# One layer of a hybrid decoder on one core: the first transfers held to three at a time

## The chip, the core and the metric

The kernel runs on one core of one Trainium2 chip. The metric is device microseconds of one execution. Before the change three runs gave 461.85, 461.92 and 461.99 us, median 461.92. The engines named below are TensorE (PE; its weight loads are PEld), VectorE (DVE), ScalarE (ACT), GpSimd (POOL) and SyncE (SP), whose queue issues nearly all transfers.

## The reference, cut to what matters

```
proj = x @ w_in                                  # 256 x 2048 by 2048 x 6656, split in nine parts
q_mo, k_mo = rope(q_mo), rope(k_mo)              # rotary from `positions`
y_mo = causal_softmax_attention(q_mo, k_mo, v_mo) * silu(g_mo)      # 8 heads x 128
y_gm = gelu(u) * (tril(W_s) @ layer_norm(gelu(v)) + b_s) * silu(g_gm)   # 4 groups x 128
mem_k, mem_v = split(mem @ w_mem_kv)             # 256 memory tokens, 2048 x 1024
y_me = softmax_attention(q_me, mem_k, mem_v) * silu(g_me)           # 4 heads x 128
out = layer_norm(ALPHA * x + concat(y_mo, y_gm, y_me) @ w_out)
```

All data are float32. With 256 positions there is one block of keys, so the block-sparse attention is plain causal attention.

## The kernel before

Every large product is computed with operands split into a high part `hi` (rounded by ACT, `split`, lines 106 to 108) and a rest `lo = raw - hi` (DVE, line 108); the products hi·hi, lo·hi and hi·lo are added up in PSUM.

The weights come as one stream of pieces in the order in which TensorE uses them (`STREAM`, line 41). The first item, "H", is `mem @ w_mem_kv` for the values: 16 pieces, one for each 128 rows of the contraction. A piece of H (array `head`) holds 256 columns of the transposed memory and 512 columns of weights, 128 x 768 floats, 384 KB. `load_piece` (lines 135 to 157) takes a buffer of the tag `wraw` (six of them, shared by `hraw` and `wraw`), has SP issue the transfer, and splits both halves: ACT makes `memX` hi (line 150; DVE for the first piece, line 148) and `whi`, DVE makes `memX` lo (line 151) and `wlo`. `whi` and `wlo` have four buffers each.

`next_pieces` (line 191) calls `load_piece` for the piece that is due and three more (`LEAD`). `proj_n` (line 220) runs six matmuls of 512 columns for each piece of H, in the order hi·hi, hi·lo of the memory, lo of the weights, for two token tiles (lines 242 to 246). Then `proj_t` (line 202) computes four blocks of `mem_k` from the same memory; in those calls a hook (line 441) loads the eight pieces of `xT` (`load_act`, line 172, 256 KB each, split into `xX`) and, once, calls `rotary()` (line 273), which loads `pos` and `inv_freq` and computes the tables `sinT` and `cosT` with some twenty DVE instructions and two ACT sines. `xX` and the tables are used only after those four blocks. The rest is the input projections, the attention, the gate units and the output projection with its layer norm.

Before the first piece TensorE runs seven matmuls on zeros (`N_WARM`, line 121).

What sets the order on each engine is not the text alone. The kernel is written for a framework that traces it and then orders all instructions itself: it runs through them with its own estimates of time and lets each engine take the ready instruction that stands first in the text; where the next one in the text is not ready by its estimate, a later one may go first. It also places all semaphore waits and gives tiles their buffers. Each engine then runs its own list strictly in that order.

Of the kernel before, what the change touches and what calls it, by code (L numbers as in the profile page):

```python
# [9 lines left out]
F32 = mybir.dt.float32  # L10
# [7 lines left out]
P = 128  # L18
S = 256
D = 2048  # L20
KT = D // P
# [33 lines left out]
PIECE = 1024  # L55
LEAD = 3
N_WARM = 7


def pieces_of(item):  # L60

    if item[0] == "H":
        return KT, 1, item[3]
    width = P if item[0] == "T" else item[3]
    kts = PIECE // width
    return KT // kts, kts, width
# [14 lines left out]
def hymba_layer(ctx: ExitStack, tc: tile.TileContext, xT, head, x, pos, inv_freq, w, wsT, b_s,  # L81
                gln_g, gln_b, ln_g, ln_b, out):
    nc = tc.nc

    def pool(name, bufs, space=None):
        kw = {"space": space} if space is not None else {}
        return ctx.enter_context(tc.tile_pool(name=name, bufs=bufs, **kw))
# [3 lines left out]
    wp = pool("wp", 1)  # L91
# [8 lines left out]
    def f32(ap):  # L100
        return ap.bitcast(F32)
# [4 lines left out]
    def split(hi, lo, src):  # L106
        nc.scalar.activation(hi, src, AF.Copy)  # L107
        nc.vector.tensor_tensor(out=lo, in0=src, in1=f32(hi), op=ALU.subtract)  # L108
# [10 lines left out]
    idle = ps_side.tile([P, NW], F32, tag="side", name="idle")  # L119
    for _ in range(N_WARM):  # L120
        nc.tensor.matmul(idle, zero[:, :P], zero, start=True, stop=True)
# [3 lines left out]
    for i, item in enumerate(STREAM):  # L125
        n, kts, width = pieces_of(item)
# [3 lines left out]
    for n, (i, j, _, _) in enumerate(pieces):  # L130
        if j == 0:
            first_piece[i] = n
    ready = {}

    def load_piece(n):
        if n >= len(pieces) or n in ready:
            return
        i, j, kts, width = pieces[n]
        if i == len(STREAM) - 1 and j > LEAD:
            hi, lo = (held_home(j - LEAD - 1, b).rearrange("p (k n) -> p k n", k=kts) for b in range(2))  # L140
        else:
            hi = wp.tile([P, kts, width], F32R, tag="whi", name="whi", bufs=LEAD + 1)
            lo = wp.tile([P, kts, width], F32R, tag="wlo", name="wlo", bufs=LEAD + 1)
        if STREAM[i][0] == "H":
            both = wp.tile([P, PIECE], F32, tag="wraw", name="hraw", bufs=6)[:, :S + width]
            nc.sync.dma_start(both, head[j])
            if j == 0:
                nc.vector.tensor_copy(memX[:, j, 0, :], both[:, :S])
            else:
                nc.scalar.activation(memX[:, j, 0, :], both[:, :S], AF.Copy)  # L150
            nc.vector.tensor_tensor(out=memX[:, j, 1, :], in0=both[:, :S], in1=f32(memX[:, j, 0, :]), op=ALU.subtract)
            split(hi[:, 0, :], lo[:, 0, :], both[:, S:])
        else:
            raw = wp.tile([P, kts, width], F32, tag="wraw", name="wraw", bufs=6)
            nc.sync.dma_start(raw, w[n - KT].rearrange("p (k n) -> p k n", k=kts))
            split(hi, lo, raw)
        ready[n] = (hi, lo)
# [3 lines left out]
    def held_home(m, b):  # L161

        if m < 2:
            return outX[0][:, 2 * m + b, :]
        tag, pool_ = (("mv", act), ("pT", work))[m - 2]
        return pool_.tile([P, 2, NW], F32R, tag=tag, name="held", bufs=2).rearrange("p a n -> p (a n)")
# [24 lines left out]
    def next_pieces(hook=None):  # L191
        i = item[0]
        item[0] += 1
        n, kts, width = pieces_of(STREAM[i])
        for j in range(n):
            for m in range(LEAD + 1):
                load_piece(first_piece[i] + j + m)
            if hook is not None:
                hook(j)
            yield j, kts, ready.pop(first_piece[i] + j)  # L200
# [430 lines left out]
```

## Time and profile before

| | us |
|---|---|
| median of three runs | 461.92 |
| the profiled execution | 462.48 |
| its span, first to last instruction | 460.8 |
| PE busy in the span | 447.7 |
| DVE, ACT busy | 343.1, 231.4 |

TensorE is busy for 97% of the span; its own work and the short start and end around it make up the time. The profiled execution takes 1.7 us more than its span, and 0.56 us more than the median of the runs. Times in the trace are microseconds from the start of the span. The column of the granted clock reads 1.00 in the first microseconds, where the trace has no record of it.

### The profile page before, as it was taken

How to read it: one execution, taken by the hardware profiler on the slowest of the kernel's cores; microseconds unless marked ns; L12 is line 12 of the kernel's file. 1: busy time of each engine (PE TensorE's matmuls, PEld its weight loads, DVE VectorE, ACT ScalarE, POOL GpSimd, SP SyncE). 2: the span in 40 equal slices, each digit the busy share in tenths (PEclk: the TensorE clock that was granted, in tenths of full speed). 3: DMA queues.
4: the chain of work that ended last, by engine and by line, in shares of the span. 5: the costliest groups of instructions: out<-in, count | busy, mean ns of one | idle time of the engine just before them, and what ended most of it. 6: DMA issues, size and time to landing. Idle time of an engine off the chain costs nothing.

```text
span 460.8 us, 6498 instructions
## 1 busy us (share of the span) xinstructions
PE 447.7 (97%) x2367; PEld 381.9 (83%) x2367; DVE 343.1 (74%) x592; ACT 231.4 (50%) x369; POOL 6.6 (1%) x17
## 2 busy tenths in 40 slices
PE   8999999999999999999999999999999999999990
PEld 4888888888888888888888888888888888888880
DVE  5989865777577988885678888867987746466666
ACT  5876854575444555554455455445655543336200
POOL 1000000000000000000000000000100000000000
PEclk9999999999999999999999999999999999999996
DMA  8988786544455445544555455966464557676122
GB/s 286 351 338 301 269 273 229 164 166 148 158 197 181 163 170 184 182 160 169 195 185 177 168 184 174 313 213 214 158 213 177 184 191 236 205 231 209 70 91 91
DMA packets 28543, 91.77 MB, mean 199 GB/s; under 512 B 3296, under 2 KB 3424, under 8 KB 28512
## 3 DMA queue, kind: packets, MB, share of 16 engines
q1 hardware_dynamic: 27936, 90.32, 56.7%
q10 hardware_dynamic: 576, 1.05, 0.6%
q8 instruction: 18, 0.29, 0.2%
q14 instruction: 13, 0.11, 0.1%
HBM read 89.26 MB, written 2.10 MB: 198 GB/s over the span
## 4 chain that ended last, share of the span: by engine, by line
PE 96%; DMA 1%; DVE 1%; ACT 0%; issue 0%; SPq 0%; DVEq 0%
PE acc L210 36%; PE acc L211 18%; PE acc L112 11%; PE acc L114 11%; PE acc L113 11%; PE acc L245 4%; DMA hraw<-head 1%; PE ptp L405 1%; PE sc L112 1%; DVE hX L557 0%; DVE hX L553 0%; PE pv L114 0%; PE sc L113 0%; PE pv L113 0%; PE sc L114 0%; PE pv L112 0%
## 5 line engine op out<-in xcount | busy, mean ns | idle before, releaser
L108 DVE TENSOR_TENSOR wlo<-wraw,whi 128x1024 fp32r<-128x1024 f32 x140 | 171.3, 1224 | 79.8 <-ACT whi L107 78.6
L210 PE MATMUL acc<-xX,whi 128*128 128x512 f32 x640 | 227.3, 398 | 0.0
L107 ACT ACTIVATE whi<-wraw 128x1024 fp32r<-128x1024 f32 x140 | 148.3, 1059 | 150.4 <-PE acc L210 60.3
L211 PE MATMUL acc<-xX,wlo 128*128 128x256 f32 x640 | 179.4, 280 | 0.0
L210 PEld LDWEIGHTS acc<-xX,whi 128*128 128x128 f32 x640 | 120.1, 188 | 27.8
L211 PEld LDWEIGHTS acc<-xX,wlo 128*128 128x128 f32 x640 | 120.9, 189 | 0.1
L112 PE MATMUL acc<-whi,yX 128*128 128x512 f32 x112 | 43.6, 389 | 0.0
L114 PE MATMUL acc<-wlo,yX 128*128 128x512 f32 x112 | 43.6, 389 | 0.0
L113 PE MATMUL acc<-whi,yX 128*128 128x512 f32 x112 | 43.6, 389 | 0.0
L112 PE MATMUL acc<-whi,xX 128*128 128x512 f32 x96 | 38.1, 396 | 0.0
L114 PE MATMUL acc<-wlo,xX 128*128 128x512 f32 x96 | 37.5, 391 | 0.0
L113 PE MATMUL acc<-whi,xX 128*128 128x512 f32 x96 | 37.5, 390 | 0.0
L114 PEld LDWEIGHTS acc<-wlo,yX 128*128 128x128 f32 x112 | 21.0, 188 | 4.4
L113 PEld LDWEIGHTS acc<-whi,yX 128*128 128x128 f32 x112 | 21.0, 188 | 4.4
L112 PEld LDWEIGHTS acc<-whi,yX 128*128 128x128 f32 x112 | 21.0, 188 | 4.3
L210 PE MATMUL acc<-memX,whi 128*128 128x512 f32 x64 | 22.6, 399 | 0.0
L114 PEld LDWEIGHTS acc<-wlo,xX 128*128 128x128 f32 x96 | 18.0, 188 | 3.9
L112 PEld LDWEIGHTS acc<-whi,xX 128*128 128x128 f32 x96 | 18.1, 188 | 3.4
L113 PEld LDWEIGHTS acc<-whi,xX 128*128 128x128 f32 x96 | 18.1, 188 | 3.4
L245 PE MATMUL acc<-whi,memX 128*128 128x512 f32 x64 | 17.8, 400 | 0.9 <-ACT whi L107 0.9
L217 DVE TENSOR_TENSOR projT<-acc,part 128x256 f32<-128x256 f32 x44 | 18.1, 414 | 0.0
L211 PE MATMUL acc<-memX,wlo 128*128 128x256 f32 x64 | 18.0, 281 | 0.0
(149 smaller groups left out, 448.6 us busy)
## 6 DMA issues: line engine op xcount, KB each, us to landing
wraw<-weights SPq DMA_DIRECT2D x144, 512.0 KB, 3.3
hraw<-head SPq DMA_DIRECT2D x16, 384.0 KB, 4.9
araw<-xT SPq DMA_DIRECT2D x8, 256.0 KB, 4.1
xs<-xrow SPq DMA_DIRECT2D x8, 256.0 KB, 4.2
lnp<-ln_gv SPq DMA_DIRECT2D x4, 256.0 KB, 4.2
lnp<-ln_bv SPq DMA_DIRECT2D x4, 256.0 KB, 4.7
out<-hX ACTq DMA_DIRECT2D x4, 256.0 KB, 2.6
out<-hX SPq DMA_DIRECT2D x4, 256.0 KB, 2.7
```

Source lines behind the costliest of these rows:

```text
L107: nc.scalar.activation(hi, src, AF.Copy)
L108: nc.vector.tensor_tensor(out=lo, in0=src, in1=f32(hi), op=ALU.subtract)
L112: nc.tensor.matmul(o, a[0], b[0], start=start, stop=False)
L113: nc.tensor.matmul(o, a[1], b[0], start=False, stop=False)
L114: nc.tensor.matmul(o, a[0], b[1], start=False, stop=stop)
L210: nc.tensor.matmul(flat, hi[:, m, :], rows(X, k).rearrange("p a s -> p (a s)"), start=k == 0, stop=False)
L211: nc.tensor.matmul(acc[:, 0, :], lo[:, m, :], rows(X, k)[:, 0, :], start=False, stop=k == KT - 1)
L217: nc.vector.tensor_tensor(out=r, in0=acc[:, 0, :], in1=part, op=ALU.add)
L245: nc.tensor.matmul(acc[t], X[:, k, a, tk[t]], b[:, m, :], start=k == 0 and a == 0 and b is hi, stop=k == KT - 1 and b is lo)
L405: nc.tensor.transpose(tp[:, n, :], st["p"][:, at[t] // P + b, :], ident)
```

## The change

Two constants, and a gate in `load_piece`. The buffers of the first four pieces of H are taken together, and then one more ahead with each piece. After the transfer of piece j is issued, DVE copies one column of piece j's buffer into the buffer of piece j + 3 (for j from 0 to 5). The copy needs piece j landed, and the transfer of piece j + 3 overwrites the copied column, so it has to wait for the copy.

```diff
+FLYING = 3
+GATED = 6
-    ready = {}
+    ready, hraw = {}, {}
         if STREAM[i][0] == "H":
-            both = wp.tile([P, PIECE], F32, tag="wraw", name="hraw", bufs=6)[:, :S + width]
-            nc.sync.dma_start(both, head[j])
+            for m in range(0 if j == 0 else FLYING, min(FLYING + 1, KT - j)):
+                hraw[j + m] = wp.tile([P, PIECE], F32, tag="wraw", name="hraw", bufs=6)
+            nc.sync.dma_start(hraw[j][:, :S + width], head[j])
+            if j < GATED:
+                nc.vector.tensor_copy(hraw[j + FLYING][:, :1], hraw[j][:, :1])
+            both = hraw.pop(j)[:, :S + width]
```

The lists of the engines come out in another order. On SP, the first rows of the list before; `hraw_108`, `hraw_116`, `hraw_124`, ... are the pieces 0, 1, 2, ... of H:

```order
L146 DMA hraw_108<-head 128x768
L146 DMA hraw_116<-head 128x768
L146 DMA hraw_124<-head 128x768
L146 DMA hraw_132<-head 128x768
L146 DMA hraw_146<-head 128x768
L146 DMA hraw_160<-head 128x768
```

The same place of SP's list now; `hraw_108`, `hraw_109`, `hraw_110`, `hraw_111` are the pieces 0 to 3, `hraw_120` and `hraw_129` the pieces 4 and 5, and `araw` are pieces of `xT`:

```order
L150 DMA hraw_108<-head 128x768
L181 DMA araw_367<-xT 128x512
L282 DMA posi_371<-pos 128x256
L284 DMA invf_373<-inv_freq 128x1
L150 DMA hraw_109<-head 128x768
L150 DMA hraw_111<-head 128x768
L181 DMA araw_424<-xT 128x512
L181 DMA araw_458<-xT 128x512
L150 DMA hraw_110<-head 128x768
L150 DMA hraw_120<-head 128x768
L181 DMA araw_484<-xT 128x512
L181 DMA araw_518<-xT 128x512
```

Before, all 16 pieces of H stand ahead of everything else. Now five of the eight pieces of `xT`, `pos` and `inv_freq` stand between the pieces of H, and piece 3, which has to wait for the copy of piece 0, stands ahead of piece 2.

On DVE, the first rows on the pieces before (after the memsets):

```order
L148 CAST memX_86<-hraw_108 128x256
L151 TENSOR_TENSOR memX_86<-hraw_108,memX_86 128x256
L108 TENSOR_TENSOR wlo_107<-hraw_108,whi_106 128x512
L151 TENSOR_TENSOR memX_86<-hraw_116,memX_86 128x256
L108 TENSOR_TENSOR wlo_115<-hraw_116,whi_114 128x512
```

And now; `ang`, `angm` and the like belong to `rotary()`, `xX0` to the activations:

```order
L152 COPY hraw_111<-hraw_108 128x1
L155 CAST memX_86<-hraw_108 128x256
L158 TENSOR_TENSOR memX_86<-hraw_108,memX_86 128x256
L299 CAST ang_375<-posi_371 128x256
L300 TENSOR_SCALAR ang_375<-ang_375,invf_373 128x256
L111 TENSOR_TENSOR wlo_107<-hraw_108,whi_106 128x512
L111 TENSOR_TENSOR xX0_87<-araw_367,xX0_87 128x2x256
L152 COPY hraw_120<-hraw_109 128x1
L296 TENSOR_SCALAR angm_376<-ang_375 128x256
L158 TENSOR_TENSOR memX_86<-hraw_109,memX_86 128x256
L297 TENSOR_SCALAR angm_376<-angm_376 128x256
L111 TENSOR_TENSOR wlo_119<-hraw_109,whi_118 128x512
```

Nearly all of `rotary()` and five splits of `xX` now lie between the splits of H, on ACT too (the five high parts and the load of the sine table); before, they came after all of H. TensorE's own list is the same as before, instruction for instruction, and from the fifth block of the projections on so are the lists of the other engines.

## Rows read from the trace of the kernel before

**Rows 1.** The page: busy time of each engine, share of the span
```profile
PE 447.7 (97%) x2367; PEld 381.9 (83%) x2367; DVE 343.1 (74%) x592; ACT 231.4 (50%) x369; POOL 6.6 (1%) x17
```
**Rows 2.** PE in four stretches: length, PE busy, granted clock, DMA share, GB/s
```profile
449.88:460.80 10.92, 0.00 (x0) 0.63 0.28 96
0.00:1.25 1.25, 0.00 (x1) 1.00 0.00 0
4.42:4.60 0.18, 0.00 (x0) 1.00 0.70 171
8.05:8.78 0.73, 0.00 (x1) 1.00 1.04 408
```
**Rows 3.** Waits of PE from 8.8 to 449 us: total, times, longest
```profile
PE acc L245 <- ACT whi L107: 0.7, 1, 0.7
```
**Rows 4.** The chain that ended last, first 40 us: start, length, what
```profile
1.70 6.06 DMA hraw<-head
...
7.79 0.42 ACT memX L150
...
8.78 19.32 PE acc L245 x84
```
**Rows 5.** SP's issues of pieces 0 and 5: start, length
```profile
0.80 0.38 SPq L146 DMA_DIRECT2D hraw<-head  x1
...
3.12 0.43 SPq L146 DMA_DIRECT2D hraw<-head  x1
```
**Rows 6.** Pieces 0, 2 and 5 of H: KB, us from issue to landing
```profile
hraw<-head SPq DMA_DIRECT2D x1, 384.0 KB, 3.1
...
hraw<-head SPq DMA_DIRECT2D x1, 384.0 KB, 6.1
...
hraw<-head SPq DMA_DIRECT2D x1, 384.0 KB, 7.6
```
**Rows 7.** Sizes of the other transfers that are moved
```profile
araw<-xT SPq DMA_DIRECT2D x7, 256.0 KB, 4.3
posi<-pos SPq DMA_DIRECT2D x1, 128.0 KB, 6.7
```
**Rows 8.** Stretches of 1 us: busy PE, PEld, DVE, ACT, POOL; clock, DMA share, GB/s
```profile
1.00:2.00 1.00, 0.75 (x2) 0.28 (x3) 0.21 (x3) 1.00 (x1) 0.96 (x4) 1.00 0.27 49
...
5.00:6.00 1.00, 1.00 (x4) 0.81 (x4) 0.89 (x3) 0.78 (x2) 0.00 (x0) 1.00 0.84 200
```
**Rows 9.** Short DVE instructions in the first 30 us: busy, mean ns
```profile
L148 DVE CAST memX<-hraw 128x256 fp32r<-128x256 f32 x1 | 0.3, 295 | 2.7 <-DMA hraw<-head 2.7
...
L347 DVE MEMSET rsq<- 128x1 f32 x2 | 0.1, 59 | 0.0
```
**Rows 10.** DVE by time, one piece: start, length
```profile
13.32 0.42 DVE L151 TENSOR_TENSOR memX<-hraw,memX 128x256 fp32r<-128x256 f32 x1
13.65 0.69 DVE L108 TENSOR_TENSOR wlo<-hraw,whi 128x512 fp32r<-128x512 f32 x1
14.27 0.42 DVE L151 TENSOR_TENSOR memX<-hraw,memX 128x256 fp32r<-128x256 f32 x1
```
**Rows 11.** DVE from 31 to 53 us, of the work that is moved
```profile
L108 DVE TENSOR_TENSOR xX<-araw,xX 128x512 fp32r<-128x512 f32 x8 | 5.5, 685 | 0.0
L286 DVE SCALAR_TENSOR_TENSOR ang<-angm,ang 128x256 f32<-128x256 f32 x5 | 2.1, 421 | 0.0
...
L289 DVE TENSOR_SCALAR angm<-ang 128x256 f32<-128x256 f32 x1 | 0.3, 295 | 0.0
```
**Rows 12.** PE by time at the start: start, length
```profile
1.25 3.17 PE L121 MATMUL idle<-zero 128*128 128x512 bf16 x7 [1.25 <-DVE rsq L347]
...
6.50 1.08 PE L245 MATMUL acc<-whi,memX 128*128 128x512 f32 x4
```
**Rows 13.** Stretches after the last matmul, columns as in rows 8
```profile
450.00:452.00 2.00, 0.00 (x0) 0.00 (x0) 1.90 (x5) 0.00 (x0) 0.04 (x1) 1.00 0.00 0
452.00:454.00 2.00, 0.00 (x0) 0.00 (x0) 2.00 (x4) 0.00 (x0) 0.89 (x1) 0.66 0.00 0
```

## The prediction, written before the run

> **What bounds the kernel now.** I read the busy shares first, then the stretches in which TensorE is idle, its waits, the chain that ended last, and the first microseconds by time. TensorE is busy for 97% of the span [rows 1]. All of its idle time lies in four places: 1.25 us before its first matmul, 0.18 us and 0.73 us between the first pieces of H, and 10.92 us after its last matmul [rows 2]. From 8.8 us to the end it waits once, and that is the wait which ends at 8.78 [rows 3]. The chain shows what came before 8.78: piece 2 of H is issued at 1.70, lands 6.06 us later at 7.8, ACT splits it, and from then on the chain is TensorE alone [rows 4]. So for this change one number decides: when TensorE starts piece 2 and then never stops again. If this moment moves by d, and no new wait comes later, the time moves by d.
>
> **Why piece 2 lands at 7.8.** Pieces 0 and 5 are issued at 0.80 and 3.12, five issues apart, so SP needs 0.46 us for each [rows 5]. Pieces 0, 2 and 5 land 3.1, 6.1 and 7.6 us after their issue, at 3.9, 7.8 and 10.7 [rows 6]: in the order of issue. Bytes begin to move between 1 and 2 us, and from 5 to 6 us only 200 GB/s move although the DMA engines are busy for 0.84 of it; at 8 us it is 408 GB/s at a share of 1.04 [rows 2, 8]. So there is a slow stretch, and the rest goes at full rate.
>
> **What the change does to the order.** By the text only the gate is new. But the lists come out otherwise: SP issues piece 0, then a piece of `xT`, `pos`, `inv_freq`, piece 1, and then piece 3, which waits for the copy of piece 0; behind it stand two more pieces of `xT`, and only then piece 2. SP is strictly in order, so piece 2, which needs no gate, waits behind the gate of piece 3.
>
> **Step 1, when piece 2 is issued.** SP issues five transfers from 0.80 on at 0.46 us each, the fifth at 2.6, and waits for piece 0 to land at 3.9 [rows 5, 6]. The copy of one column has no row; the nearest are a memset of one column, 59 ns, and the cast of 256 columns, 295 ns [rows 9]; I take 0.1 us, and the other end would move all this by 0.2. Piece 3 goes out at about 4.1, then two of `xT`, and piece 2 at 4.1 + 3 x 0.46 = 5.5, against 1.70 before. Queued behind the gate are all later transfers too; they are in step 4.
>
> **Step 2, when piece 2 lands.** What has to go through the queue up to piece 2 was three pieces of 0.393 MB, 1.18 MB. Now it is four pieces of H, three of `xT` of 0.262 MB and `pos` with 0.131 MB [rows 7]: 1.57 + 0.79 + 0.13 = 2.49 MB. The queue doesn't run dry ahead of it: pieces 0 and 1 with what lies between them are 1.18 MB too, which before had landed only at 7.8, and by 5.5 piece 3 and two of `xT` are queued behind them.
> - Lower end: no slow stretch. Piece 0 lands at 3.9 as before, and the other 2.10 MB follow at 0.408 MB a us [rows 2], 5.1 us: 9.0.
> - Upper end: the pace of before with its slow stretch. 2.36 MB had landed at 10.7, and 0.13 MB more take 0.3 us: 11.0.
> - I take the middle, 10.0: the slow stretch is one row, and nothing in the trace ties it to the number of transfers under way.
>
> **Step 3, when TensorE starts piece 2.** From the landing to the first matmul it took 1.0 us before (7.77 to 8.78: two ACT instructions) [rows 4]. Ahead of them on ACT now stand two splits of `xT` pieces, but these landed earlier in the same queue, and 0.6 us each is done while piece 2 lands. So TensorE starts piece 2 at 11.0 instead of 8.78: +2.2 us. (Lower end 10.0, +1.2; upper end 12.0, +3.2.) The later start of piece 1 (a landing some 1 to 2 us later) lies inside this, since TensorE would wait for piece 2 anyway.
>
> **Step 4, what is late next.** From piece 2 on TensorE takes 1.38 us a piece (19.32 us for 84 matmuls, 6 a piece) [rows 4].
> - DVE. One piece takes 0.33 for `memX` lo and 0.62 for `wlo`, start to start [rows 10]; instructions overlap by 0.08. The moved work costs 0.60 for a split of `xX`, 0.34 and 0.21 for the rotary steps by the same overlap [rows 11]. From the landing of piece 2 to the last `wlo` DVE has 14 x 0.62 + 13 x 0.33 + 2 x 0.60 + 8 x 0.34 + 4 x 0.21 + 4 copies x 0.1 = 18.1 us. TensorE needs that `wlo` 1.0 + 13 x 1.38 + 0.92 = 19.9 us after the landing. Slack 1.8 us: DVE keeps up, though it loses nearly all its idle time.
> - Piece 5 is issued only when piece 2 has landed and DVE has copied from it, then queues behind piece 4 and two of `xT`: 2 x 0.393 + 2 x 0.262 = 1.31 MB after piece 2, which take 3.2 us at 0.408 MB a us and 4.5 us at the pace of before (1.97 MB from 3.9 to 10.7). TensorE needs it landed 1.0 + 3 x 1.38 - 1.0 = 4.1 us after piece 2. Slack 0.9 or -0.4: I take the first, since the slow stretch is then over, and keep 0.4 for the range.
> - What leaves the stretch from 28 to 52 us (five transfers, the rotary work, a table load on ACT) gives nothing back: TensorE never waits there [rows 3].
>
> **Sum.** The profiled execution: span 460.8 + 2.2 = 463.0, with the 1.7 us around it 464.7. The median of the runs is 0.56 below that execution: 464.1 us. A change under 0.2%, 0.92 us, can't be told from none here.
>
> **Rivals.**
> *Not slower (0.10).* The place is the transfer stretch up to piece 2. If the slow stretch comes from six transfers at once, it goes with the gate, and piece 0 comes earlier too: 2.49 MB at 0.408 from 1.8 us on have moved at 7.9 [rows 2, 8], and between that and the lower end of 9.0 piece 2 lands at about 8.5, TensorE starts it at 9.5, +0.7 us, 462.6. It decides from a landing under 8.7. For it: six transfers are under way when the rate falls. Against: at 8 us nearly as many are, and the rate is full [rows 2]. The Trainium skill ("DMA: Bandwidth & Descriptors", Latency and other measured facts) says that the access latency of HBM rises from 0.2 us on average to 2 us at high load, which speaks for this rival; the trace is slow at 5 us but at full rate at 8 us under nearly the same load, so it bears this out by half. By that rule the sum would be the 462.6 just given.
>
> *The clock falls back (0.15).* TensorE now has 1.4 us of work on piece 1 and then some 2.5 us of nothing. At the lower level a matmul of 512 columns takes 3.17 / 7 = 0.45 us, at the higher 1.08 / 4 = 0.27 with its end, 0.23 start to start [rows 12]. That is 1.2 and 2.4 GHz. It was at the lower level from 1.25 to at least 4.4, and at the higher by 6.5; if these 3.2 to 5.2 us come once more behind the gap, half of them is lost, some 2.1 us: 464.1 + 2.1 = 466.2. Against: after the last matmul, at 449.9, the granted clock still reads 1.00 up to 452 and falls within the next 2 us [rows 13], later than the gap lasts; but there TensorE had been busy without a break before it. The Trainium skill ("TensorE: Matmul & The Clock Gate", HAM oscillation) says that a wait for data between bursts of matmuls can put the gate back and that the next burst then starts cold. The trace has no such gap inside the work.
>
> *DVE becomes the bound (0.10).* If the rotary steps cost their wait on each other as well (they depend on one another, and I gave them the overlap of independent ones), or if ACT's order makes DVE wait, the slack of 1.8 us is used up and TensorE waits for `wlo` at the end of H: some 1.5 us more, 465.6. For it: nearly every rotary step stands between two splits that TensorE needs.
>
> *The gate does nothing (in the forecast's lower half).* If transfers simply drain in order, holding three back can't bring pieces 0 to 2 forward, and what remains is the new order alone; that is what the sum is made of.
>
> **How the numbers follow.** The forecast, +1.2 to +3.2 us, has 0.65, and its own range is 463.1 to 465.1. The rivals have 0.10, 0.15 and 0.10. The range of 462.6 to 466.4 takes in half of the first and nearly all of the other two, and leaves out some 0.15 in all. Faster by over 0.2%: 0.03, since even the first rival's price is later than before. Within 0.2%: 0.09, with the upper half of the first rival and a little of the forecast. Slower: 0.88.
>
> **What would show it.** In the changed profile: SP's issues of `hraw` broken up, the fourth after 4 us; piece 2 landing between 9.0 and 11; the wait of TensorE before it 2 to 3 us long instead of 0.73; after it no wait up to the end of H; DVE full from 9 to 28 us; the granted clock 1.00 there. Wrong if TensorE starts piece 2 before 9.7, if a second wait of over 0.5 us shows up inside H or at its end, or if the stretch after 60 us takes another time than before.

## The result and the profile after

The changed kernel takes 469.55 us, the median of six runs (468.17 to 471.16), against 461.96 us before on the same chip (461.72 to 462.48): a ratio of 1.0164, with a 95% interval of 1.0147 to 1.0181. It is slower by 7.6 us. The profiled execution took 469.85 us, and what answers to [rows 1] is this, from its page:

```profile
span 468.1 us, 6508 instructions
...
PE 449.6 (96%) x2367; PEld 382.0 (82%) x2367; DVE 343.4 (73%) x598; ACT 231.4 (49%) x369; POOL 7.6 (2%) x17
```

The span is 7.3 us longer, and TensorE's busy time grew by only 1.9. The rest is waiting. Its waits are (total, how often, longest):

```profile
PE acc L252 <- DVE wlo L111: 4.4, 1, 4.4
PE acc L252 <- ACT whi L110: 1.5, 2, 1.2
...
PE acc L252 <- DVE memX L158: 0.4, 1, 0.4
```

All waits on line 252 lie inside H; they add up to 6.3 us, against 0.9 before. TensorE by time, start and length, the idle time before in brackets:

```profile
4.47 1.19 PE L252 MATMUL acc<-whi,memX 128*128 128x512 f32 x4
10.07 1.22 PE L252 MATMUL acc<-wlo,memX 128*128 128x512 f32 x2 [4.41 <-DVE wlo L111]
11.09 1.99 PE L252 MATMUL acc<-whi,memX 128*128 128x512 f32 x4
12.88 1.05 PE L252 MATMUL acc<-wlo,memX 128*128 128x512 f32 x2
14.19 0.85 PE L252 MATMUL acc<-whi,memX 128*128 128x512 f32 x2 [0.26 <-ACT whi L110]
...
24.97 1.20 PE L252 MATMUL acc<-whi,memX 128*128 128x512 f32 x4 [1.21 <-ACT whi L110]
```

The four matmuls at 4.47 are the high part of piece 0. The low part of the same piece comes only at 10.07. Piece 1 follows at 11.09 and piece 2 at 14.19 (before: 8.78 [rows 4]), which is 5.4 us later; the wait just before it is 0.26 us. Piece 8 at 24.97 is 7.9 us later than before.

Why the low part of piece 0 is so late is seen on DVE, by time:

```profile
4.18 0.43 DVE L158 TENSOR_TENSOR memX<-hraw,memX 128x256 fp32r<-128x256 f32 x1
7.95 0.29 DVE L299 CAST ang<-posi 128x256 f32<-128x256 int32 x1 [3.34 <-DMA posi<-pos]
9.06 0.35 DVE L300 TENSOR_SCALAR ang<-ang,invf 128x256 f32<-128x256 f32 x1 [0.82 <-DMA invf<-inv_freq]
9.33 0.68 DVE L111 TENSOR_TENSOR wlo<-hraw,whi 128x512 fp32r<-128x512 f32 x1
```

Piece 0 had been in memory since 3.8. Its `wlo` stands in DVE's list behind two rotary steps, and these wait for `pos` until 7.95 and for `inv_freq` until 9.06. SP's issues from the second on, and then size and time from issue to landing of the first transfers (up to 13 us), which answer to [rows 5 to 7]:

```profile
1.24 0.42 SPq L181 DMA_DIRECT2D araw<-xT  x1
1.70 0.43 SPq L282 DMA_DIRECT2D posi<-pos  x1
2.17 0.43 SPq L284 DMA_DIRECT2D invf<-inv_freq  x1
2.65 1.65 SPq L150 DMA_DIRECT2D hraw<-head  x2
4.34 2.08 SPq L181 DMA_DIRECT2D araw<-xT  x2
6.46 4.58 SPq L150 DMA_DIRECT2D hraw<-head  x2
```

```profile
hraw<-head SPq DMA_DIRECT2D x5, 384.0 KB, 6.7
araw<-xT SPq DMA_DIRECT2D x4, 256.0 KB, 5.8
posi<-pos SPq DMA_DIRECT2D x1, 128.0 KB, 6.2
invf<-inv_freq SPq DMA_DIRECT2D x1, 0.5 KB, 6.8
```

The half kilobyte of `inv_freq` lands 6.8 us after its issue, behind all that was issued before it: `pos` lands at 7.92 and `inv_freq` at 8.96. The same stretches of 1 us as in [rows 8] tell more (last three columns: granted clock, DMA share, GB/s):

```profile
4.00:5.00 1.00, 0.91 (x3) 0.48 (x3) 0.57 (x2) 0.91 (x2) 0.00 (x0) 1.00 0.23 76
5.00:6.00 1.00, 0.66 (x3) 0.19 (x1) 0.00 (x0) 0.14 (x1) 0.00 (x0) 1.00 0.34 95
6.00:7.00 1.00, 0.00 (x0) 0.00 (x0) 0.00 (x0) 0.00 (x0) 0.00 (x0) 1.00 0.65 237
7.00:8.00 1.00, 0.00 (x0) 0.00 (x0) 0.05 (x1) 0.00 (x0) 0.00 (x0) 0.82 0.91 335
```

At 4 us pieces 1 and 3 of H and one of `xT` are issued and have not landed, yet from 4 to 6 us only 76 and 95 GB/s move, and the DMA engines are busy for a quarter to a third of the time. Before, the slowest of these stretches between 2 and 10 us moved 200 GB/s [rows 8]. And the clock: TensorE has been idle since 5.66, and from 7.6 on the granted clock reads 0.50, the lower of the two levels; it is back only at 14.5, so the rest of piece 0, piece 1 and the start of piece 2 run at 1.2 GHz. The end of H is told by the chain of waits that ended last:

```profile
2.17 6.79 DMA invf<-inv_freq
...
9.33 0.68 DVE wlo L111
...
14.09 0.60 DVE xX L111
14.69 0.09 DVE hraw L152 x2
14.78 3.33 DMA hraw<-head
...
18.83 5.06 DMA hraw<-head
...
24.30 0.62 ACT whi L110
...
24.97 11.21 PE acc L252 x48
```

In place of piece 2's landing [rows 4], the chain begins with `inv_freq` and goes through DVE's list (splits and rotary steps in one row from 9.3 to 14.7) to DVE's copies from pieces 2 and 3 (`hraw L152`), which run at 14.6 though piece 2 landed at 13.2. Only then is piece 5 issued, at 14.78. It lands at 18.1, DVE copies from it at 18.61, and piece 8 goes at 18.83, too late.

### The profile page after: what moved, and what is told of

Its sections match the earlier page's. It is cut to its first block, busy times and chain, and to the rows that moved or that the text cites. A ratio compares the mean times of both kernels' runs of the same rounds, so it can differ in the third digit from the quotient of the medians.

```text
span 468.1 us, 6508 instructions
## 1 busy us (share of the span) xinstructions
PE 449.6 (96%) x2367; PEld 382.0 (82%) x2367; DVE 343.4 (73%) x598; ACT 231.4 (49%) x369; POOL 7.6 (2%) x17
## 3 DMA queue, kind: packets, MB, share of 16 engines
q10 hardware_dynamic: 576, 1.05, 0.6%
## 4 chain that ended last, share of the span: by engine, by line
PE 92%; DMA 3%; DVE 2%; issue 1%; SPq 0%; ACT 0%; DVEq 0%; ACTq 0%
PE acc L217 35%; PE acc L218 18%; PE acc L115 11%; PE acc L117 11%; PE acc L116 11%; PE acc L252 2%; DMA hraw<-head 2%; DMA invf<-inv_freq 1%; PE ptp L412 1%; PE sc L115 0%; DVE hX L564 0%; DVE hX L560 0%; PE pv L117 0%; PE sc L116 0%; PE pv L116 0%
## 5 line engine op out<-in xcount | busy, mean ns | idle before, releaser
L116 PEld LDWEIGHTS acc<-whi,xX 128*128 128x128 f32 x96 | 18.1, 188 | 3.4
L252 PE MATMUL acc<-whi,memX 128*128 128x512 f32 x64 | 18.8, 415 | 1.9 <-ACT whi L110 1.5
```

Source lines behind the costliest of these rows:

```text
L116: nc.tensor.matmul(o, a[1], b[0], start=False, stop=False)
L252: nc.tensor.matmul(acc[t], X[:, k, a, tk[t]], b[:, m, :], start=k == 0 and a == 0 and b is hi, stop=k == KT - 1 and b is lo)
```

## Experiments

Theory A: the gate costs nothing, the new order that comes with it does, above all the two small loads near the head of the queue. Theory B: the gate starves the queue, and that costs. A helper in these kernels: what stands under `behind_h()` is put behind the last piece of H on its engine (with `False` it holds nothing back).

**1. The gate without the new order (g_held).** All loads of `xT`, `pos`, `inv_freq`, the rotary work and the late loads of the gate units behind H, the pieces of H in their own order:

```diff
-            nc.sync.dma_start(hraw[j][:, :S + width], head[j])
+            d = nc.sync.dma_start(hraw[j][:, :S + width], head[j])
+            tc.keep_in_program_order(d)
...
-        nc.sync.dma_start(posi, bcast(pos, S))
+        with behind_h(True):
+            nc.sync.dma_start(posi, bcast(pos, S))
...
-            load_act(xT, xX, 4 * h + 2 * j, 2)
+            with behind_h(True):
+                load_act(xT, xX, 4 * h + 2 * j, 2)
...
-        nc.vector.tensor_copy(a, posi)
+        with behind_h():
+            nc.vector.tensor_copy(a, posi)
...
```

> The gate on three transfers stays, but everything that had moved ahead (pieces of xT, pos, inv_freq, the rotary work, the late loads) is held in issue order behind the last piece of H, and the pieces of H are issued in their own order. Theory A (the new order is the cost, above all pos and inv_freq ahead of pieces of H, in the queue and on DVE): 461 to 462.8 us, TensorE starts piece 2 by 9 us and its waits inside H add up to 2 us at most. Theory B (the gate itself starves the transfers): at least 465 us, under 250 GB/s from 4 to 8 us and waits of TensorE of over 4 us inside H.

Measured: 462.65 us, ratio 1.0016 (1.0006 to 1.0025). Its first stretches:

```profile
4.00:5.00 1.00, 0.71 (x2) 0.29 (x2) 0.94 (x4) 0.68 (x2) 0.00 (x0) 1.00 1.02 375
5.00:6.00 1.00, 1.00 (x6) 0.78 (x6) 0.91 (x4) 0.89 (x2) 0.00 (x0) 1.00 1.01 280
...
7.00:8.00 1.00, 1.00 (x6) 0.84 (x5) 0.86 (x3) 0.38 (x2) 0.00 (x0) 1.00 0.75 221
```

The queue does run below its full rate with three pieces under way (221 GB/s at 7 to 8 us), but TensorE hardly waits for it: piece 2 starts at 7.58, and one wait of 0.6 us comes at piece 9. Theory B explains 0.7 us of 7.6, and 1.2 at the interval's end. The gate also does what it was made for: piece 2, issued at 1.71, lands 4.5 us later, at 6.2, where before it took 6.1 us and landed at 7.8 [rows 6].

```profile
hraw<-head SPq DMA_DIRECT2D x1, 384.0 KB, 4.5
```

By piece 9 this is lost again.

**2. The parts of the order, with the gate.** From g_held, one part at a time is let go again, and the scheduler places it: four pieces of `xT` (g_xfirst; three of them come ahead of piece 1 and the fourth ahead of piece 2, so not quite the places of the changed kernel); `pos`, `inv_freq` and the rotary work (g_rotfirst); all these loads, with the rotary work alone held (g_loadsfirst). In g_xfirst:

```diff
-            with behind_h(True):
+            with behind_h(False):
                 load_act(xT, xX, 4 * h + 2 * j, 2)
```

> The gate, and of what had moved only four pieces of xT and their splits go ahead; pos, inv_freq and the rotary work are held behind H. Theory A: bytes alone, 1.05 MB at about 0.4 MB a us: piece 2 lands at 8 to 9.5 us, TensorE starts it 0.5 to 2 us later than before the change, 462.5 to 464 us. A theory that the bytes of xT are the cost: 467 us or more.

> The gate, and of what had moved only pos, inv_freq and the rotary work go ahead; the pieces of xT are held behind H. Theory A: most of the loss is here, 466 to 470 us; inv_freq lands at 7 us or later, DVE waits for it for 3 us or more in front of the first lo, and TensorE with it. A theory that the bytes of xT are the cost: under 463.5 us. Theory B: as the run with everything held, at least 465, with no wait of DVE for pos or inv_freq above 1 us.

> The gate, and the loads of xT, pos and inv_freq go ahead, but the rotary work on DVE and ACT is held behind H, so DVE never waits for pos or inv_freq ahead of a lo. If the queue behind the two small transfers is the cost: piece 1 still lands at 8 us or later and the time is 465 to 469 us. If DVE's place in its list is the cost: 462.5 to 464.5 us, and TensorE's first wait is under 2 us.

Measured: g_xfirst 466.29 us (ratio 1.0099, 1.0082 to 1.0116), g_rotfirst 468.99 (1.0154, 1.0138 to 1.0169), g_loadsfirst 467.53 (1.0133, 1.0108 to 1.0157). Each part alone costs half of the loss or more, so the parts don't add up. Theory A missed on g_xfirst: it had 462.5 to 464, so the small loads are not the whole cost of the order. There piece 2 landed at 10.45 and TensorE started it at 11.46, 2.7 us later than before; then the granted clock read 0.50 from 9.48 to 12.89, and H ended 3.5 us later. g_rotfirst came within its range, but `inv_freq` landed at 6.48 there and DVE waited only 1.6 us for the two loads, not 3. From g_loadsfirst to the changed kernel it is another 2.0 us by the medians: there the rotary work stands between the splits, and piece 3 ahead of piece 2. The wait for the low part of piece 0 shows up only where the rotary work is early; in g_loadsfirst TensorE waits for the landing of piece 1 instead (4.1 us, on ACT's `whi`).

**3. The order without the gate (b_loads).** From the kernel before: `xT`, `pos`, `inv_freq` behind piece 0, two of `xT` behind piece 1, as in g_loadsfirst, and no gate; rotary work behind H.

```diff
             nc.sync.dma_start(both, head[j])
+            if j == 0:
+                early_x(0)
+                early_loads()
+            if j == 1:
+                early_x(1)
+                early_x(2)
...
```

> The kernel before without any gate, with SP's order of the gated run that was 467.5 us (piece 0, a piece of xT, pos, inv_freq, piece 1, two pieces of xT, piece 2 and so on); the splits of these three pieces of xT stand between those of H, the rotary work behind H. Theory D (order alone): 466.5 to 467.5 us, as with the gate. Rival (gate and order together are what costs): 464.5 to 465.5 us, namely 1.5 us for pos and inv_freq and 0.65 us for each of the three pieces of xT of which two stand ahead of piece 2.

Measured: 467.36 us, ratio 1.0120 (1.0098 to 1.0142): the same as with the gate. The queue stands still in the same place though all buffers of H may be filled:

```profile
4.00:5.00 1.00, 1.00 (x3) 0.58 (x3) 1.00 (x3) 0.91 (x2) 0.00 (x0) 1.00 0.28 57
5.00:6.00 1.00, 1.00 (x6) 0.68 (x4) 0.63 (x2) 0.00 (x0) 0.00 (x0) 1.00 0.44 81
```

This settles the order against the gate: the order of the loads alone costs 5.3 us, the gate on top of it 0.2 us by the medians, with intervals that overlap.

**4. The two small loads by themselves.** From the kernel before, without gate, behind piece 0: only `pos` (b_pos), only `inv_freq` (b_inv), both (b_posinv); both with the gate (g_posinv, which is g_held with these two loads let go).

```diff
             nc.sync.dma_start(both, head[j])
+            if j == 0:
+                early_loads()                # posi, invf or both
...
-                rotary()
+                with behind_h():
+                    rotary()
```

> The kernel before without any gate; only pos (128 copies of one 1 KB row, 128 KB written) is issued right behind piece 0 of H; inv_freq, xT and the rotary work stay behind H. Theory A2 (pos blocks the queue): a stretch under 100 GB/s between 4 and 6 us, piece 2 lands 1 to 2.5 us later, TensorE starts it at 9.8 to 11.3: 463.0 to 464.5 us (up to 465.5 with the clock). Theory A1 (inv_freq blocks): 0.46 us for the issue and 0.3 us for the bytes, TensorE starts piece 2 at 9.3 to 9.6: 462.5 to 462.8. Theory B (bytes): the same 462.5 to 462.8.

> The kernel before without any gate; only inv_freq (512 B, 4 B a partition) is issued right behind piece 0 of H, ahead of piece 1; pos, xT and the rotary work stay behind H. Theory A1 (this load, not the gate and not the bytes, holds up the queue): SP issues it at 1.2 us, the rate of the queue falls below 100 GB/s somewhere between 4 and 6 us, pieces 1 and 2 land some 1 to 2 us later, TensorE starts piece 2 at 9.8 to 10.8 instead of 8.8: 463.0 to 464.0 us (with the fall of the clock up to 465). Theory A2 (pos is the one that blocks): +0.5 us, one more issue on SP: 462.5. Theory B (bytes alone): no more than that issue, 462.0 to 462.5.

> The kernel before without any gate; pos and inv_freq together are issued right behind piece 0, xT and the rotary work stay behind H. Alone they moved TensorE's pieces by 1.05 (pos) and 0.5 us (inv_freq). If they add up: TensorE starts piece 2 about 1.5 us later, at 10.3, 463.5 to 464.5 us. If the stall is worse with both in the queue (as the changed kernel's rates of 76 and 95 GB/s from 4 to 6 us suggest): 2.5 to 3.5 us later, 465 to 466.

> The same two loads right behind piece 0, but with the gate of six, pieces in their own order, xT and the rotary work behind H. If the gate makes the stall dearer (only three pieces are in the queue behind the small loads, so nothing else moves while those wait): later than the same without the gate by 1 us or more, 465.5 to 467. If the gate is free here too: the same as without it within 0.5 us. And against the run in which the rotary work stands between the pieces as well (468.99 us): what is missing from it here is the price of DVE's list.

Measured: b_pos 463.60 us (1.0046, 1.0030 to 1.0062), b_inv 463.31 (1.0039, 1.0021 to 1.0057), b_posinv 467.09 (1.0108, 1.0087 to 1.0128), g_posinv 465.69 (1.0091, 1.0067 to 1.0115). Both loads delay the queue; by bytes they would cost 0.3 us and nothing. By the medians `pos` costs 1.5 us, `inv_freq` 1.2, both 5.0 (3.6 with the gate, which is neither outcome of the expectation; the interval overlaps that of b_posinv, so the gate can't be said to help). In the profiles, one for each kernel, all of H moves by 1.05 us for `pos`, 0.5 for `inv_freq`, and 3.2 for both; the profiled execution of b_posinv, 465.71, is the fastest of its four, so 1.4 us of its median stand in no profile, and that of b_inv has a single wait of 2.1 us for `projT` after H.

g_posinv has a second use. It differs from g_rotfirst (468.99 us) in the rotary work alone: same loads, pieces of H in their own order, but the rotary steps behind H. The difference is 3.3 us, with intervals that don't overlap; H ends 2.6 us later in g_rotfirst. That is the price of the rotary steps in DVE's list. The `wlo` of piece 0 runs there at 7.96, behind steps that wait for `pos` and `inv_freq`:

```profile
7.96 0.68 DVE L111 TENSOR_TENSOR wlo<-hraw,whi 128x512 fp32r<-128x512 f32 x1
```

and in g_posinv at 4.52:

```profile
4.52 0.69 DVE L111 TENSOR_TENSOR wlo<-hraw,whi 128x512 fp32r<-128x512 f32 x1
```

The stretches of b_posinv:

```profile
4.00:5.00 1.00, 1.00 (x3) 0.61 (x3) 0.98 (x2) 0.25 (x1) 0.00 (x0) 1.00 0.37 40
5.00:6.00 1.00, 1.00 (x5) 0.82 (x4) 0.00 (x0) 0.00 (x0) 0.00 (x0) 1.00 0.39 127
```

And with `pos` alone in the same place:

```profile
4.00:5.00 1.00, 0.79 (x2) 0.37 (x2) 0.97 (x3) 0.58 (x1) 0.00 (x0) 1.00 0.45 116
```

A part of why both cost twice their sum is seen on TensorE. With `pos` alone:

```profile
8.45 1.19 PE L260 MATMUL acc<-whi,memX 128*128 128x512 f32 x4 [2.06 <-ACT whi L107]
```

and with both:

```profile
9.13 2.07 PE L262 MATMUL acc<-whi,memX 128*128 128x512 f32 x4 [2.60 <-ACT whi L107]
11.01 1.05 PE L262 MATMUL acc<-wlo,memX 128*128 128x512 f32 x2
11.86 1.33 PE L262 MATMUL acc<-whi,memX 128*128 128x512 f32 x4
```

The start of piece 1 is late by 1.95 (`pos`), 1.04 (`inv_freq`) and 2.63 us (both), and the landing of piece 2 by 0.65, 0.47 and 1.30: nearly plain sums. But with both the first four matmuls of piece 1 take 2.07 us instead of 1.19: in that wait the granted clock fell to 0.50 (from 8.97 to 12.38), with one load alone it did not.

**5. Both small loads on ACT's own queue (b_actq).** As b_posinv, but issued by ACT at 0.80 and 1.24; `inv_freq` is changed likewise.

```diff
-        tc.keep_in_program_order(nc.sync.dma_start(rot["posi"], bcast(pos, S)))
+        tc.keep_in_program_order(nc.scalar.dma_start(rot["posi"], bcast(pos, S)))
...
```

> The kernel before without any gate, pos and inv_freq first on ACT's own DMA queue at 0.8 us (at the same time as piece 0 on SP's), rotary work and xT behind H. If it is the place in SP's queue that matters (later transfers of a queue stand behind its small ones): no shift beyond bytes, TensorE starts piece 2 at 8.8 to 9.2, 462.0 to 462.6 us. If the small pieces of data hold up the DMA engines themselves, whatever the queue: as with both on SP's queue, 463.5 us or more.

Measured: 465.10 us, ratio 1.0074 (1.0057 to 1.0090). The other queue saves 2.0 us against b_posinv and still costs 3.0: now piece 0 itself, alone at the head of SP's queue, lands at 6.1 instead of 3.9, as DVE's first use of it shows.

```profile
6.13 0.29 DVE L152 CAST memX<-hraw 128x256 fp32r<-128x256 f32 x1 [4.92 <-DMA hraw<-head]
```

So it isn't only the place in one queue; something that the two queues share is held up.

**6. The clock (a_warm, b_posinv_w22, b_loads_w26).** The changed kernel, b_posinv and b_loads with more warm-up matmuls, which fill TensorE's wait:

```diff
-N_WARM = 7
+N_WARM = 27        # a_warm; 22 in b_posinv_w22, 26 in b_loads_w26
```

> The changed kernel with 27 warm-up matmuls instead of 7, so that TensorE is busy from 1.2 to some 9 us and has only a short gap before the low part of piece 0 comes at 10.0. Theory C (the fall of the clock is a symptom here: the landings and DVE's list decide, piece 2 lands at 13.2 and piece 8 at 23.9 whatever the clock is): the granted clock stays 1.00, TensorE works through pieces 0 and 1 faster and then waits longer, pieces 2 and 8 start as in the changed kernel, 469.0 to 469.7 us. Rival (the clock itself costs): the matmuls from 10.1 to 14.5 at half speed are paid, 1.5 to 2 us come back, 467.5 to 468.

> As the run with pos and inv_freq right behind piece 0 and no gate (467.09 us, in its profiled execution 465.71), but with 22 warm-up matmuls instead of 7, which fill most of TensorE's wait for piece 1. Theory (the fall of the clock is what the two loads cost beyond the sum of each alone): the granted clock stays at 1.00, piece 1 starts at 9.1 to 9.3 as without it, the pieces 1 and 2 take 1.4 us each instead of 2.7 and 1.6, piece 3 starts at 11.9 to 12.2 instead of 13.5: 1.3 to 1.6 us come back, 464.2 to 465.8. Rival (the landings decide anyway): no change, 465.7 to 467.

> As the run with the changed order of the loads and no gate (467.36 us), but with 26 warm-up matmuls instead of 7, which fill TensorE's wait for piece 1. Theory (the clock is a part of the cost of the order): clock 1.00, piece 1 starts at 10.0 as without, piece 2 at 12.0 to 12.3 instead of 12.7 (its split on ACT is late by then), piece 3 at 13.4 to 13.7 instead of 15.2: 1.5 to 1.8 us come back, 465.5 to 466. Rival (the landings decide anyway): 467 to 467.5.

Measured: b_posinv_w22 464.82 us (1.0055, 1.0038 to 1.0072) against 467.09; b_loads_w26 466.56 (1.0088, 1.0067 to 1.0110) against 467.36; a_warm 468.22 (1.0139, 1.0111 to 1.0166) against 469.55. The clock reads 1.00 in the gap in all three. Of b_posinv_w22:

```profile
9.60 1.20 PE L262 MATMUL acc<-whi,memX 128*128 128x512 f32 x4
10.64 0.62 PE L262 MATMUL acc<-wlo,memX 128*128 128x512 f32 x2
11.10 1.07 PE L262 MATMUL acc<-whi,memX 128*128 128x512 f32 x4
```

Piece 1 starts even a little later than at 9.13, piece 2 0.8 us earlier, and all of H from there on 1.0 us earlier: it ends 2.2 us later than before, where b_posinv's ends 3.2 later. In b_loads_w26 H is earlier by 1.8 us, of which a later wait of 0.9 us for a `wlo` takes back half; in a_warm piece 2 starts 1.4 us earlier and H ends 1.3 earlier. Of the totals only that of b_posinv_w22 is clear of noise; the intervals of the other two overlap with those of their counterparts. So the clock is worth 1 to 2 us in H, and theory C, by which it costs nothing, missed. It is a part of the loss and not its cause: with the clock at 1.00 most of it stays.

**7. Two gates only (g_held2).** As g_held, with `GATED = 2`:

```diff
-GATED = 6
+GATED = 2
```

> The gate with the order of before (all other transfers behind H), but only two gates instead of six: pieces 3 and 4 wait for pieces 0 and 1, from piece 5 on none waits. Theory: three at a time brings pieces 0 to 2 forward (piece 2 starts at 7.6 instead of 8.8, as with six gates), and without the later gates the queue is full again after 7 us, so that the wait at piece 9 (2.2 us with six gates) gets shorter or goes: 461.0 to 461.9 us, at most 0.9 us faster than before. Rival: the rate lost while only three are under way (221 to 304 GB/s at 5 to 8 us) is not made up, a piece between 6 and 10 is late by what was gained: 462.0 to 462.7, no different from six gates.

Measured: 461.94 us, ratio 0.9999 (0.9990 to 1.0009). The wait at piece 9 is gone (it was 0.6 us; the 2.2 of the expectation is the distance from the start of piece 8), and piece 2 lands at 6.0, but nothing is gained over before that is clear of noise. No version was found that beats the kernel before.

## Why the prediction was wrong

The direction was right, and so was the order in which SP issues. The size was 7.6 us instead of 2.2, and the place was only half right. TensorE did start piece 2 late, by 5.4 us, but the long wait of 4.4 us lies inside piece 0, with 0.26 us before piece 2, and the condition of the sum, no new wait after that, failed. Against the forecast of 2.2 us, piece 2 landed 3.2 us later than forecast (step 2), after the start of piece 2 another 2.7 us were lost up to the end of H (step 4), and 0.7 us net came back after H (last section). Two of the named signs of being wrong came: a second wait of over 0.5 us inside H (1.2 us at piece 8), and a stretch after 60 us that takes another time, 0.6 us less.

- **Step 1 held nearly.** Piece 3 was issued at 4.0 (forecast 4.1); the copy takes 0.15 us. Piece 2 was issued at 6.46 instead of 5.5, since the two issues of `xT` before it took 2.08 us and not 0.92.
- **Step 2 failed, and this is the first cause.** It sized the queue by bytes: `pos` as 0.13 MB, `inv_freq` as nothing. Piece 2 landed at 13.2 instead of 9.0 to 11.0. With four pieces of `xT` ahead of it and no small load (g_xfirst) it landed at 10.45, so their bytes fit the step. With the small loads and the pieces of H in their own order (g_loadsfirst) it landed at 11.57, though a piece less of H stands ahead of it. The runs put in place of the bytes a price for each small load: 1.05 and 0.5 us of H for 128 rows of 1 KB and of 4 bytes, 2.6 us of piece 1 for both, with a stretch of 40 to 127 GB/s. The sign of it stood in the trace before, where both loads pass the queue behind H:

```profile
27.00:28.00 1.00, 1.00 (x6) 0.81 (x5) 0.79 (x2) 0.55 (x2) 0.00 (x0) 1.00 0.56 169
```

  The rate falls to 169 GB/s at a share of 0.56, with weights queued behind; in b_posinv, where both loads are gone from there, the same stretch moves 332 GB/s. Nobody waits for them there, so the stall cost nothing, and I took a load without a wait for a load without a price. The Trainium skill ("DMA: Bandwidth & Descriptors", Bandwidth) says that transfers under 64 KB are dominated by their descriptors; for `inv_freq` the trace agrees in so far as its 0.5 KB cost 0.5 us of H. By its table, made with another issuing engine and counting only the time in which the DMA engines are busy, 4 KB take 0.68 us; here 0.5 KB landed 4.0 us after their issue in b_inv and 6.8 us after it in the changed kernel, with the wait behind earlier transfers in both. The same page of the Trainium skill (Specifications) wants at least 512 B for full rate, which the 1 KB rows of `pos` have, and still the rate fell to 116 GB/s; there the measurement decides.
- **Step 2 also misread the pace of before.** It took the pieces to move one after the other: 1.18 MB by 7.8 us, with a slow stretch. In that time the queue of the kernel before moved 268 GB/s for 6.77 us, 1.8 MB:

```profile
1.00:7.77 6.77, 6.34 (x19) 3.42 (x19) 2.65 (x8) 2.64 (x4) 1.15 (x4) 1.00 0.83 268
```

  So 0.6 MB of the pieces issued later had moved before the last of piece 2. In the changed kernel it was 3.0 MB by 13.18, not the 2.49 of the sum.
- **Step 3 was right in its own term** (1.0 us from landing to TensorE, measured 1.0), but it looked at pieces and not at DVE's list. The 4.4 us wait for the low part of piece 0 is in no term of the sum, although the order shown ahead of the prediction has the rotary steps in front of that `wlo`. I asked how much work DVE gets, not what its first moved instruction waits for.
- **Step 4 failed on DVE.** The slack of 1.8 us was counted from the landing of piece 2 with DVE free by then. DVE took up its row at 9.33 instead of 4.6, nearly 5 us behind, released gates and buffers late, and piece 8 came 1.2 us after TensorE wanted it. With the rotary work behind H (g_loadsfirst) no such wait comes, and the time is 2.0 us better; that run also has pieces 2 and 3 in their own order. The rotary work by itself, with the pieces in their own order and without the early `xT`, is the 3.3 us between g_posinv and g_rotfirst. That the later stretch gives nothing back held but for 1.0 us (below).
- **The rivals.** "Not slower" didn't come: in the changed kernel the slow stretch got slower. But its mechanism isn't out. With the gate alone (g_held) the stretches from 4 to 6 us move 375 and 280 GB/s, before 280 and 200, and piece 2 lands 1.6 us earlier. Whether the latency named there has a part in it no run here shows. "The gate does nothing" was right for the time, as experiments 1 and 3 show, but not for its reason: holding three back does bring piece 2 forward, and a later piece pays for it. "The clock falls back" and "DVE becomes the bound" both happened, on top of the forecast and not instead of it; I had given each a chance of its own and none to their sum, so that the range ended at 466.4. The Trainium skill's rule ("TensorE: Matmul & The Clock Gate", HAM oscillation) is borne out by rows: idle from 5.66, the clock at 0.50 from 7.6 on. My counter-evidence, the slow fall after the last matmul [rows 13], came after 440 us without a break and didn't carry over.

Of the 7.6 us the runs share out, roughly: 5.3 for the order of the loads (1 to 2 of it the clock), 0.2 or nothing for the gate, 2.0 for the rotary work on DVE's list together with piece 3 ahead of piece 2. These are not fixed prices: by the medians `xT` alone costs 4.2 us, the two small loads alone 5.0 (3.6 with the gate), and all of them together 5.3.

## What to carry to other kernels

When a change lets a scheduler move work, ask of each moved instruction what it waits for and who stands behind it in its engine's list and in the DMA queue, before asking how long it takes. Price a small load by what a trace shows of it, not by its bytes, and look at the rate of the queue where it passes now, even where nobody waits. Don't take the order in which transfers land for the order in which their bytes move: here holding transfers back brought an early one forward and cost a later one as much. Where several delays fall on one gap of TensorE, don't treat them as rivals: a longer gap can cost the clock too, and then they add up to more than their sum.

## What was not expected of the hardware

- With `pos` and a load of 512 bytes on 128 partitions in the queue, the DMA engines moved 28 GB/s from 4 to 5 us in g_posinv at a busy share of 0.39, with pieces 1 and 2 of H issued and not landed. Put on ACT's queue, the two loads still delayed SP's first piece by 2.2 us. What inside the engines holds the large transfers up was not tried, nor whether it is the length of the rows, or that `pos` reads one row 128 times.
- The rise of the clock at the start is not fixed: the profiled executions have it between 4.0 us (b_inv) and 9.8 us (b_actq), and in g_held2 at 7.3, where piece 2 starts a microsecond later than in g_held though it lands a little earlier. Shifts of less than that in the start of a piece in a single profile (piece 2 at 7.58 in g_held, the 0.5 us of `inv_freq`) shouldn't be read as an effect of an edit without the landing beside them.
- After the late start, the matmuls of the blocks after H ran a little faster in the changed kernel. The 54 of 512 columns on `memX` between 40 and 88 us take 391 ns in the mean, the 53 between 32 and 80 us before 399 ns, in the same order of instructions and at the same granted clock, and by 90 us 1.0 us of the delay have come back (8.4 at 37 us, 7.35 from 90 us to the end). In b_loads and a_warm it is 399 again. The cause stays open.
- Single waits of 0.9 to 2.1 us after H (for `projT` in b_inv, for a `wlo` in g_rotfirst and in b_loads_w26) came in some profiles and not in others; they widen the spread of these runs, and their cause was not looked for.
